# Batch norm after a matmul: w loaded by single blocks of k, x's first chunk by halves of k

## The chip, the cores and the metric

The kernel runs on one core of a Trainium2 chip. The metric is the device time of one execution in microseconds (us), beside a profile of one execution that gives each engine's instructions: TensorE (PE, with its weight loads listed apart as PEld), VectorE (DVE), ScalarE (ACT), GpSimd (POOL) and SyncE (SP), and the DMA engines that move data between the chip's memory (HBM) and the core's SBUF.

## The reference

```python
batch, m, k, n = 16, 512, 1024, 768          # x [16, 512, 1024], weight [1024, 768], fp32
def reference(x, weight, gamma, beta, eps):
    y = np.matmul(x, weight)
    mean = np.mean(y, axis=(0, 1), keepdims=True)
    var = np.var(y, axis=(0, 1), keepdims=True)
    y_norm = (y - mean) / np.sqrt(var + eps)
    return (gamma * y_norm + beta).astype(np.float32)
```

So 8192 rows of x times a 1024 x 768 matrix, and then each of the 768 columns normalised over all 8192 rows. No column of the output can be written before all rows of that column are known.

## The kernel before

**Tiling.** The 8192 rows are 16 chunks (C) of 512 rows (CH), each of two halves (QPC) of 256 rows (QR). The 768 columns are six tiles of 128 (NT). The first two tiles (GA = 2, 256 columns, NA) are called rows: for them x is the stationary operand, a group of 128 rows is multiplied with 256 columns of w, and the result has rows on the partitions. The other four tiles are called columns: w is stationary and 512 rows stream past. The contraction over k = 1024 is cut in four quarters of 256 (KQ), one on each group of 32 partitions, and inside a quarter in four blocks of 64 (jw, JW = 4) of two elements each side by side (e). One product over all of k is thus eight matmuls, two for each block. Block jw needs all four quarters of w's block jw, and all four quarters of x's block jw.

**Loading.** POOL issues the loads of w and x, which turn fp32 into bf16 on the way. One load moves one quarter: 32 partitions. `load_w(jw, jw1, quarters)` loads some blocks of w into `w_sb` (L387), `load_x(m0, rows, slot, between)` loads rows of x into a slot of `ring` (L403), four loads each. The ring holds three chunks. At most eight of POOL's loads are under way: each new one waits until the load eight places before it has landed (DMA lanes 0 to 7, used in turn). Before, the order is: w blocks 0 and 1 (quarters 0, 1), the first 256 rows of x, w blocks 0 and 1 (quarters 2, 3; the table `BETWEEN`), the next 256 rows, w blocks 2 and 3, then chunk 1 by 256 rows, and chunks 2 to 15 by 512 rows, the last in two pieces.

**Transposes.** `turn_x` (L428, L435) turns a slot of the ring on DVE into `xT_sb`, with k on the partitions. For chunk 0 this is done by halves of the rows and halves of k (two blocks), four transposes of [128 x 512 words]; the other chunks are turned by halves of the rows alone.

**Products.** `mm_rows` (L510) makes the rows tiles, `mm` (L575) the columns tiles. For chunk 0, `part(0, 1, [0, 1])` multiplies the first 256 rows with blocks 0 and 1, `part(1, 2, [0, 1])` the next 256, and then blocks 2 and 3 follow for all 512 rows. `wake` (L591) makes products of a tile of zeros, eight ahead of everything (`WAKE`), followed by eight small ones, and one (`FILL`; two passes in the profile) between the two parts. Chunk 1 has all its rows products and then all its columns products.

**After a product.** For the rows tiles ACT squares the result (L659), DVE adds it to a sum (L662), POOL or DVE adds the squares (L666), and ACT keeps a bf16 copy (L672). For the columns tiles DVE or ACT takes statistics (L711, L720, L724), and a bf16 copy is kept (L715). ACT makes plain copies of some chunks of x for faster streaming (`x_pl`, L547). When all rows of a tile are known, it is normalised, turned where needed (on PE, L1044, or in SP's DMA transposes) and stored by SP. The last tile's statistics are complete after PE's last product of y (L753); its normalisation (L1348), turning, copies (L1361) and stores (L1364) are the tail.

**The order.** Every piece of work is a `Task` with a priority, the engines that may do it with planned times (time the engine is held, time until the result is there), and its inputs and buffers. `arrange` places them one by one: at each step the engine that can begin earliest takes, of the tasks that could begin within 0.2 us, the one with the first priority. `Wires` plans the DMA. The order that comes out is what each engine executes; the planned times act through the order alone. On the chip an engine goes through its own list in order and waits where an input is missing. The waits themselves are put in by the framework, from the regions of memory that instructions write and read.

Of the kernel before, what the change touches and what calls it, by code (L numbers as in the profile page):

```python
# [9 lines left out]
class Task:  # L10
# [3 lines left out]
    def __init__(self, prio, engines, emit, deps=(), dma=None, uses=(), takes=()):  # L14
        self.prio, self.engines, self.emit, self.deps = prio, engines, emit, list(deps)
        self.dma, self.uses, self.takes = dma, list(uses), list(takes)
        self.end = self.after = None
        self.hosts = 0
        self.count = 1
        self.lock = False  # L20
        self.slack = self.look = 0.0
        for slot in self.uses + self.takes:
            slot.users.append(self)
# [74 lines left out]
class Wires:  # L98
# [4 lines left out]
    def __init__(self):  # L103
        self.free = 4.3
        self.lanes = {"SP": [], "POOL": [], "ACT": []}
# [5 lines left out]
    def send(self, queue, t, hold, took, count):  # L111

        soft = queue == "POOL"
        for _ in range(count):
            t = max(t, self.ready(queue)) + hold / count
            self.free = max(self.free, t + (1.0 if soft else 0.5)) + took / count
            land = self.free + (1.3 if soft else 0.6)
# [4 lines left out]
def arrange(tasks, turns, log=None):  # L122
# [8 lines left out]
    SEM, LOOK = 0.06, 0.2  # L131
# [36 lines left out]
    while left:  # L168
# [46 lines left out]
        if t.dma:  # L215
            free[e], t.end = wires.send(e, start, occ, t.dma, t.count)
# [11 lines left out]
def kernel(  # L228
# [30 lines left out]
    FILL = 1  # L259
    SMALL = 8  # L260
    TOUCH = 1
    BETWEEN = {0: [0, 1]}
# [112 lines left out]
    STORE, XBAR = 1 / 350.0, 1.25  # L375
# [64 lines left out]
    order = [("x", 0), ("w", 0, 2), ("x", 1), ("w", 2, 4)]  # L440
    order += [("x", q) for q in range(2, SHORT * QPC)] + [("c", c) for c in range(SHORT, C - 1)]
# [6 lines left out]
    for kind, n, *n1 in order:  # L448
        if kind == "w":
            quarters = [i for i in range(4) if n > 0 or i not in sum(BETWEEN.values(), [])]  # L450
# [7 lines left out]
            continue  # L458
        rows = n1[0] if kind == "p" else QR if kind == "x" else CH
# [4 lines left out]
        between = BETWEEN if m0 == 0 else {}  # L464
        also = sum(len(v) for v in between.values())
        load = task(
            t, {"POOL": (2.68 * rows / CH + 0.535 * also, 2.68 * rows / CH + 0.535 * also)}, load_x(m0, rows, slot, between),
            dma=(rows * K * 4 / 1024 + 384 * also) * PER_KB * 1.024, takes=[slot])
        load.count = 4 + also
# [3 lines left out]
        for i in range(rows // QR):  # L473
            c, q = divmod(m0 // QR + i, QPC)
            for j0, j1 in ((0, JW // 2), (JW // 2, JW)) if m0 < CH else ((0, JW),):
                new = q == 0 and j0 == 0
                x_ready[c, q, j1] = task(
                    -1000 + t, dve((2.2 if c in SINGLE else 1.16) * (j1 - j0) / JW + 0.02),
                    turn_x(slot, x_slot[c], m0, i * QR // 32, j0, j1, new), [load],
                    uses=[slot] if new else [slot, x_slot[c]], takes=[x_slot[c]] if new else [])  # L480
                if not new:
                    x_ready[c, q, j1].deps.append(x_ready[c, 0, JW // 2 if m0 < CH else JW])
            x_ready.setdefault((c, q, JW // 2), x_ready[c, q, JW])
        if rows % QR:
# [4 lines left out]
                -1000 + t, dve(0.63), turn_x(slot, x_slot[c], m0, t0, 0, JW, False, P),  # L489
# [159 lines left out]
    def rows_stats(c, ts, slot, t):  # L649
# [30 lines left out]
        s = task((now + 4.2 if c < RC - 2 else 0), {"POOL": (1.36, 1.36 + 0.05), "DVE": (0.62, 0.7)}, add_squares, [a],  # L680
# [124 lines left out]
    def ga_unit(nt, c, q, cols=QR):  # L805
# [26 lines left out]
        b = task(clock[0] - late, dve(0.609 * cols / CH + 0.05), bn, [t], uses=[slot])  # L832
        mine = [h[1] for k, h in ga_half.items() if k[1] == c]
        k = task(clock[0] + 3.4, act(0.48 * cols / CH + 0.03), keep, [b] + mine,
                 uses=[slot] + ([y_row[c]] if mine else []), takes=[] if mine else [y_row[c]])
        ga_half[nt, c, q] = b, k

    for c in range(1, RC):
        for ts in ([0, 1], [2, 3]):
            rows_unit(c, ts)  # L840
        if c in PARTED:
            part_chunk(c, clock[0] + (4.0 if c < EARLY else 20.0), act(1.05))
        columns = ([c - 1] if 0 < c - 1 < EARLY and c - 1 in PARTED else []) + (
            [c] if c < EARLY and c not in PARTED else [])
# [10 lines left out]
    merges.append(task(U, dve(0.36), merge(0), [k[1] for k in ends], True))  # L855
    merges.append(task(U, pool(0.65), merge(1), [k[2] for k in ends]))
    for h in range(2):
        merges.append(task(U, pool(0.65), more(h), merges[1:]))
# [59 lines left out]
    s1 = task(U, pe(0.9), sums_rows, merges, takes=[tot_slot])  # L918
    se = task(U, dve(0.8), sums_entry, [s1], True, uses=[tot_slot])
    ag = [task(U, dve(0.25), aggregate_rows(a), [se] + [h[0] for k, h in ga_half.items() if k[0] == a]) for a in range(GA)]  # L920
    rt = task(U, {"ACT": (0.2, 0.3)}, root_rows, ag)
    sc = task(U, dve(0.3), scale_rows, [rt], True)
    sr = task(U + 0.1, dve(0.35), shift_rows, [sc], True)
    p0 = task(U, pe(0.45), spread_rows(0), [sc], takes=[a0_slot])
    p1 = task(U, pe(0.45), spread_rows(1), [sr], takes=[a1_slot])
    p1.look = 0.6
    sh = task(U, act(0.3), shift_sbuf, [p1], uses=[a1_slot])


    def rows_out(c, s0, s1, k):  # L930
# [19 lines left out]
        a = task(due, dve(0.3 * n), norm, [p0] + keeps, takes=[slot], uses=[y_row[c], a0_slot])  # L950
# [461 lines left out]
```

## Time and profile before

| | us |
|---|---|
| median of 3 runs (lowest, highest) | 205.97 (205.72, 206.15) |
| profiled execution, span from first to last instruction | 204.07 |
| PE busy | 189.3 (93%), 1210 products |
| DVE busy | 159.3 (78%) |
| ACT busy | 146.2 (72%) |
| POOL busy | 124.1 (61%) |
| HBM read, written | 36.71 MB, 25.17 MB |

The page cuts the span into 40 slices of 5.1 us; a digit is the busy share in tenths, PEclk the granted clock of TensorE, DMA the busy share of the 16 DMA engines:

```profile
PE   7969999999999999999999999999999999997900
DVE  4031879999999999969989998987999878657900
PEclk9999999999999999999999999999999999999965
DMA  4999999999999999999686899899999999999998
GB/s 71 172 199 196 176 196 196 196 197 197 190 193 197 197 196 196 196 197 195 103 181 200 297 339 336 248 301 328 295 322 227 336 303 274 347 343 310 310 347 253
```

The first half of the span loads x (some 196 GB/s as written in bf16, twice that as read in fp32), the second half stores. GB/s counts the bytes written.

### The profile page before, as it was taken

The page shows a single profiled execution, that of the slowest core. Times are in us where ns is not written, and L with a number is a line of the kernel's source. Part 1 is how long each engine was busy: PE and PEld are TensorE (multiplying, and loading weights), DVE is VectorE, ACT ScalarE, POOL GpSimd, SP SyncE. Part 2 cuts the span into 40 slices and gives each one's busy share as a digit, 9 for nine tenths or more (in the row PEclk, how much of TensorE's full clock was granted, in tenths as well). Part 3 has the DMA queues.
Part 4 walks back from the last instruction along what each step waited for, and adds up shares of the span by engine and source line. Part 5 has one row for each costly group of instructions (what it writes and reads, how often), then busy time and mean ns, then how long its engine had stood idle before and what let it go on. Part 6 is the DMA issues. An engine that isn't in the chain of part 4 may idle for free.

```text
span 204.1 us, 3510 instructions
## 1 busy us (share of the span) xinstructions
PE 189.3 (93%) x1210; PEld 114.5 (56%) x1210; DVE 159.3 (78%) x250; ACT 146.2 (72%) x260; POOL 124.1 (61%) x150
## 2 busy tenths in 40 slices
PE   7969999999999999999999999999999999997900
PEld 3457554657488888777865444444444445544600
DVE  4031879999999999969989998987999878657900
ACT  2001461368989999899978766999998959956950
POOL 7776954877499989997403999389613312940000
PEclk9999999999999999999999999999999999999965
DMA  4999999999999999999686899899999999999998
GB/s 71 172 199 196 176 196 196 196 197 197 190 193 197 197 196 196 196 197 195 103 181 200 297 339 336 248 301 328 295 322 227 336 303 274 347 343 310 310 347 253
DMA packets 98562, 48.74 MB, mean 239 GB/s; under 512 B 24304, under 2 KB 98032, under 8 KB 98544
## 3 DMA queue, kind: packets, MB, share of 16 engines
q0 software_dynamic: 34624, 18.36, 65.5%
q1 hardware_dynamic: 63920, 30.16, 52.6%
q8 instruction: 9, 0.15, 0.3%
q14 instruction: 9, 0.07, 0.1%
HBM read 36.71 MB, written 25.17 MB: 303 GB/s over the span
## 4 chain that ended last, share of the span: by engine, by line
PE 86%; ACT 3%; DMA 3%; POOL 2%; issue 1%; ACTq 0%; DVE 0%; POOLq 0%
PE y_ps L575 54%; PE y_ps L510 24%; PE y_ps L814 4%; ACT o_sb L1361 3%; DMA ring<-in_x_dram 3%; PE o_ps L1044 1%; POOL ring L403 1%; POOL w_sb L387 1%; PE y_ps L753 1%; PE a_ps L903 1%; PE o_ps L1074 0%; ACTq L1407 0%; PE idle_ps L591 0%; PE tot_ps L871 0%; ACT ring L1252 0%
## 5 line engine op out<-in xcount | busy, mean ns | idle before, releaser
L575 PEld LDWEIGHTS <-w_sb 128*128 128x128 bf16 x520 | 50.3, 97 | 57.6
L575 PE MATMUL y_ps<-xT_sb,w_sb 128*128 128x512 bf16 (+1 forms) x272 | 59.3, 371 | 0.0
L575 PE MATMUL y_ps<-x_pl,w_sb 128*128 128x512 bf16 x248 | 57.4, 379 | 0.0
L403 POOL DMA_DIRECT2D ring<-in_x_dram x76 | 47.2, 626 | 14.4 <-DMA ring<-in_x_dram 5.5
L510 PE MATMUL y_ps<-w_sb,xT_sb 128*128 128x256 bf16 x448 | 50.6, 273 | 1.7 <-DMA ring<-in_x_dram 1.6
L510 PEld LDWEIGHTS <-xT_sb 128*128 128x128 bf16 x448 | 43.5, 98 | 9.4 <-DVE xT_sb L435 2.9
L435 DVE STREAM_TRANSPOSE xT_sb<-ring 128x1024 f32<-128x1024 f32 (+1 forms) x29 | 31.2, 1111 | 14.1 <-DMA ring<-in_x_dram 13.9
L711 DVE BATCH_NORM_STATS2 stats<-y_ps 128x6 f32<-128x512 f32 x46 | 30.9, 687 | 7.7 <-PE y_ps L575 7.2
L715 ACT CAST y_sb<-y_ps 128x512 bf16<-128x512 f32 x51 | 29.0, 593 | 10.4 <-DVE stats L711 6.3
L547 ACT COPY x_pl<-xT_sb 128x1024 bf16<-128x1024 bf16 x32 | 32.8, 1063 | 1.7 <-DVE xT_sb L435 1.7
L942 POOL TENSOR_TENSOR ring<-ring,sum 128x1024 f32<-128x1024 f32 (+1 forms) x11 | 23.8, 2188 | 14.9 <-ACT y_ps L724 10.9
L659 ACT ACTIVATE sq_sb<-y_ps 128x512 f32<-128x512 f32 x28 | 16.3, 610 | 16.2 <-PE y_ps L510 15.9
L666 POOL TENSOR_TENSOR sum<-sum,sq_sb 128x512 f32<-128x512 f32 x20 | 25.6, 1278 | 3.0 <-ACT sq_sb L659 1.7
L662 DVE TENSOR_TENSOR sum<-y_ps,sum 128x512 f32<-128x512 f32 x28 | 18.9, 675 | 6.3 <-ACT sq_sb L659 5.3
L672 ACT CAST y_sb<-y_ps 128x512 bf16<-128x512 f32 x28 | 16.3, 594 | 8.2 <-DVE sum L662 8.0
L1178 POOL TENSOR_TENSOR ring<-ring,sum 128x1024 f32<-128x1024 f32 x6 | 14.8, 2477 | 9.8 <-issue 8.5
L937 DVE TENSOR_TENSOR ring<-y_sb,a_ps 128x1024 f32<-128x1024 bf16 (+1 forms) x16 | 16.7, 1079 | 0.1
L1044 PE MATMUL o_ps<-ident,y_sb 128*128 128x128 bf16 x104 | 13.1, 221 | 1.6 <-DVE y_sb L1348 1.5
L1232 ACT CAST ring<-ring 128x1024 f32<-128x1024 bf16 x13 | 13.8, 1063 | 0.6 <-DMA ring<-y_sb 0.6
L1145 POOL COPY sum<-sum 32x256 f32<-32x256 f32 (+1 forms) x17 | 5.8, 340 | 13.4 <-DVE sum L1142 6.5
L428 DVE STREAM_TRANSPOSE xT_sb<-ring 128x2048 bf16<-128x2048 bf16 x6 | 13.5, 2290 | 0.1
L591 PE MATMUL idle_ps<-idle_sb 128*128 128x512 f32 x18 | 9.6, 688 | 1.5 <-DVE idle_sb L316 1.5
(104 smaller groups left out, 153.7 us busy)
## 6 DMA issues: line engine op xcount, KB each, us to landing
out_dram<-ring SPq DMA_DIRECT2D x37, 512.0 KB, 3.4
ring<-in_x_dram POOLq DMA_DIRECT2D x52, 256.0 KB, 8.8
out_dram<-o_sb SPq DMA_DIRECT2D x6, 512.0 KB, 4.7
ring<-in_x_dram POOLq DMA_DIRECT2D x16, 128.0 KB, 5.9
w_sb<-in_weight_dram POOLq DMA_DIRECT2D x8, 192.0 KB, 6.2
out_dram<-ring SPq DMA_DIRECT2D x6, 256.0 KB, 3.0
ring<-in_x_dram POOLq DMA_DIRECT2D x4, 192.0 KB, 7.8
out_dram<-o_sb SPq DMA_DIRECT2D x3, 256.0 KB, 2.5
```

Source lines behind the costliest of these rows:

```text
L403: bi = seq(nc.gpsimd.dma_start(x_bf[32 * i:32 * i + 32], src[:, :, KQ * i:KQ * (i + 1)]))
L435: seq(nc.vector.transpose(dst, src[:, :, jw0:jw1]))
L510: seq(nc.tensor.matmul(y_ps[:, s], x_of(c, jw, e, t * P, (t + 1) * P), w_sb[:, jw, e, 0:NA], start=(s == 0 and jw == 0 and e == 0), stop=( ...
L547: seq(nc.scalar.copy(dst, pairs) if eng == "ACT" else ENG[eng].tensor_copy(dst, pairs))
L575: seq(nc.tensor.matmul(y_ps, w_sb[:, jw, e, nt * P:(nt + 1) * P], moving(c, jw, e, q0 * QR, q1 * QR, parted), start=(jw == 0 and e == 0 an ...
L659: seq(nc.scalar.activation(sq_sb[:, 0:n], slot.tile[:, 0:n], AF.Square))
L662: seq(nc.vector.tensor_add(sum1, slot.tile[:, 0:n], sum1))
L666: seq(ENG[eng].tensor_add(acc, acc, state["sq"][:, 0:n]))
L711: seq(nc.vector.bn_stats(dst, slot.tile))
L715: seq(nc.scalar.copy(y(nt, c), slot.tile))
L937: seq(nc.vector.tensor_mul(slot.o, y_row[c].y[:, s0:s1], aff[0][:, None, :].to_broadcast([P, n, NA])))
L942: seq(ENG[eng].tensor_add(slot.o, slot.o, row[:, None, :].to_broadcast([P, n, NA])))
```

## The change

w is loaded in four steps of one block each, four loads a step (16 loads instead of 8). Chunk 0 of x is loaded in two steps, each with all 512 rows and half of every quarter of k (blocks 0 and 1, then 2 and 3), four loads a step, into one ring slot: rows of 128 elements where there were 256. `BETWEEN` and `FILL` are gone. Chunk 0 is multiplied with block 0 by halves of the rows, then with blocks 1, 2 and 3, one at a time, over all rows. Chunk 1 is transposed by halves of the rows and of k, and multiplied half by half. The planned times of most tasks, and those of the DMA plan, take other values.

```diff
@@ class Wires
-        self.free = 4.3
+        self.free = 4.21
-    def send(self, queue, t, hold, took, count):
-        soft = queue == "POOL"
+    def send(self, queue, t, hold, took, count, turned=False):
+        if turned:
+            t = max(t, self.ready(queue))
+            self.free = max(self.free, t + 0.722) + took
+            land = max(self.free + 0.375, t + hold + 1.4)
+            self.lanes[queue].append(land)
+            return max(t + hold, land - 2.325), land
+        first, last = (1.095, 1.0425) if queue == "POOL" else (0.722, 0.441)
...
-    SEM, LOOK = 0.06, 0.2
+    SEM, LOOK = 0.03, 0.2
...
-    FILL = 1
-    BETWEEN = {0: [0, 1]}
...
-    def load_x(m0, rows, slot, between):
+    def load_x(m0, rows, slot, k0=0, k1=KQ):
         def emit(eng):
-            x_bf = piece(slot).bitcast(bf16).rearrange("p (t k) -> p t k", k=KQ)
-            slot.tile = x_bf
+            if k0 == 0:
+                slot.tile = piece(slot).bitcast(bf16).rearrange("p (t k) -> p t k", k=KQ)
             src = x_flat[m0:m0 + rows].rearrange("(t r) k -> r t k", r=32)
             for i in range(4):
-                for quarter in between.get(i, ()):
-                    load_quarter(quarter, 0, 2)
-                bi = seq(nc.gpsimd.dma_start(x_bf[32 * i:32 * i + 32], src[:, :, KQ * i:KQ * (i + 1)]))
+                bi = seq(nc.gpsimd.dma_start(
+                    slot.tile[32 * i:32 * i + 32, :, k0:k1], src[:, :, KQ * i + k0:KQ * i + k1]))
...
-    order = [("x", 0), ("w", 0, 2), ("x", 1), ("w", 2, 4)]
-    order += [("x", q) for q in range(2, SHORT * QPC)] + [("c", c) for c in range(SHORT, C - 1)]
+    order = [("w", 0, 1), ("k", 0), ("w", 1, 2), ("k", 1), ("w", 2, 3), ("w", 3, 4)]
+    order += [("x", q) for q in range(QPC, SHORT * QPC)] + [("c", c) for c in range(SHORT, C - 1)]
...
+        if kind == "k":
+            slot = Slot(rings, RT * KQ * 2) if n == 0 else slot
+            load = task(t, {"POOL": (2.6, 2.6)}, load_x(0, CH, slot, n * KQ // 2, (n + 1) * KQ // 2),
+                        dma=CH * K * 2 / 1024 * PER_KB * 1.024, **({"uses": [slot]} if n else {"takes": [slot]}))
+            load.count = 4
...
+            j0, j1 = (0, JW // 2) if n == 0 else (JW // 2, JW)
+            for q in range(QPC):
+                new = n == 0 and q == 0
+                x_ready[0, q, j1] = task(
+                    -1000 + t, dve(0.62), turn_x(slot, x_slot[0], 0, q * QR // 32, j0, j1, new),
+                    [load] + ([] if new else [x_ready[0, 0, JW // 2]]),
+                    uses=[slot] if new else [slot, x_slot[0]], takes=[x_slot[0]] if new else [])
+            continue
...
-            for j0, j1 in ((0, JW // 2), (JW // 2, JW)) if m0 < CH else ((0, JW),):
+            for j0, j1 in ((0, JW // 2), (JW // 2, JW)) if m0 < SHORT * CH else ((0, JW),):
...
-    part(0, 1, [0, 1])
-    fill_slot = Slot(banks)
-    pe_task(0.87 * FILL, wake(FILL, fill_slot), [w_ready[0]], takes=[fill_slot])
-    part(1, 2, [0, 1])
-    for h in range(2):
-        rows_unit(0, [2 * h, 2 * h + 1], [2, 3])
-    for nt in range(GA, NT):
-        col_unit(nt, 0, [2, 3])
+    for q in range(QPC):
+        part(q, q + 1, [0])
+    for jw in range(1, JW):
+        for h in range(2):
+            rows_unit(0, [2 * h, 2 * h + 1], [jw])
+        for nt in range(GA, NT):
+            col_unit(nt, 0, [jw])
...
+    for q in range(QPC):
+        for jws in halves:
+            rows_unit(1, [2 * q, 2 * q + 1], jws)
+        for nt in range(GA, NT):
+            col_unit(nt, 1, range(JW), q, q + 1)
...
-        s = task((now + 4.2 if c < RC - 2 else 0), {"POOL": (1.36, 1.36 + 0.05), "DVE": (0.62, 0.7)}, add_squares, [a],
+        s = task((now + 4.2 if c < RC - 2 else 0), {"POOL": (1.22, 1.276), "DVE": (0.60, 0.682)}, add_squares, [a],
...
-        b = task(due, {"SP": (1.4, 1.4)}, xbar, [col_end[nt, c + i][1] for i in range(GY)] + [gate], dma=XBAR,
+        b = task(due, TURN, xbar, [col_end[nt, c + i][1] for i in range(GY)] + [gate], dma=XBAR,
```

Some twenty other tasks have their planned times changed in the same manner.

More of the change, by code (lines that the diff above doesn't have):

```diff
@@ L215, in arrange @@
         if t.dma:
-            free[e], t.end = wires.send(e, start, occ, t.dma, t.count)
+            free[e], t.end = wires.send(e, start, occ, t.dma, t.count, t.turned)
         t.start, t.engine = start, e
@@ L449 @@
         if kind == "w":
-            quarters = [i for i in range(4) if n > 0 or i not in sum(BETWEEN.values(), [])]
+            quarters = range(4)
             took = len(quarters) * 192 * 4 * (n1[0] - n) / 4 * PER_KB * 1.024
@@ L463 @@
         slot = Slot(rings, rows // 32 * KQ // 2)
-        between = BETWEEN if m0 == 0 else {}
-        also = sum(len(v) for v in between.values())
         load = task(
-            t, {"POOL": (2.68 * rows / CH + 0.535 * also, 2.68 * rows / CH + 0.535 * also)}, load_x(m0, rows, slot, between),
-            dma=(rows * K * 4 / 1024 + 384 * also) * PER_KB * 1.024, takes=[slot])
-        load.count = 4 + also
+            t, {"POOL": (2.57 * rows / CH,) * 2}, load_x(m0, rows, slot),
+            dma=rows * K * 4 / 1024 * PER_KB * 1.024, takes=[slot])
+        load.count = 4
         slot.loader = load
@@ L854 @@
                 ga_unit(nt, c, q)
-    merges.append(task(U, dve(0.36), merge(0), [k[1] for k in ends], True))
-    merges.append(task(U, pool(0.65), merge(1), [k[2] for k in ends]))
+    merges.append(task(U, {"DVE": (0.489, 0.567)}, merge(0), [k[1] for k in ends], True))
+    merges.append(task(U, {"POOL": (0.70, 0.737)}, merge(1), [k[2] for k in ends]))
     for h in range(2):
-        merges.append(task(U, pool(0.65), more(h), merges[1:]))
+        merges.append(task(U, {"POOL": (0.735, 0.764)}, more(h), merges[1:]))
     S = clock[0]
@@ L1010, in finish_tasks @@
         if nt in ASTAT:
-            deps = [task(now + 1.0, {"ACT": (1.2, 1.3)}, total, deps)]
+            deps = [task(now + 1.0, {"ACT": (0.82, 0.91)}, total, deps)]
         a = task(now + 1.0, dve(0.5), var, deps)
@@ L1014, in finish_tasks @@
         if nt > GA:
[L1015 removed]
+            return task(now + 1.0, {"DVE": (0.78, 0.87)}, affine, [b], True)
         d = task(now + 1.0, dve(0.1), invert, [b])
@@ L1270 @@
             for i, c in enumerate(LATE):
-                part_chunk(c, clock[0] + 0.0 + 4.0 * i, {"DVE": (0.63, 0.7), "ACT": (1.05, 1.1)},
+                part_chunk(c, clock[0] + 0.0 + 4.0 * i, {"DVE": (0.58, 0.67), "ACT": (0.946, 1.056)},
                            i == 0, 4.0 / 4, [col_end[NT - 3, late[-1]][1]])
```

73 lines of the change are left out of this document (39 added, 34 removed).

## The prediction

> **What bounds the kernel now.** I read the page first, then the chain of waits, then the timeline of single engines over the first 30 us, then windows over the tail. The page gives PE 189.3 us busy of a span of 204.1 (93%), and the chain that ended last is 86% PE. In the chain of waits (start us, us, what) the beginning is this:
>
> ```profile
> 5.98 6.13 DMA ring<-in_x_dram
> 12.11 0.03 issue
> 12.14 1.03 PE y_ps L510 x8
> 13.17 1.81 PE y_ps L575 x16
> 14.99 0.86 PE idle_ps L591 x2
> 15.85 0.87 PE y_ps L510 x8
> 16.72 1.81 PE y_ps L575 x16
> 18.54 0.07 issue
> 18.61 1.91 PE y_ps L510 x16
> 20.51 3.61 PE y_ps L575 x16
> 24.12 1.76 PE y_ps L510 x16
> ...
> 186.62 0.24 PE o_ps L1044 x4
> ```
>
> The first real product starts at 12.14, and from there to 186.62 the chain stays on PE, with 0.07 and 0.04 us between pieces. So the span is: start of PE's work, plus PE's work, plus a tail of 204.07 - 186.62 = 17.45 us. Inside lies 0.86 us of idle products. PE's waits, in total, times, longest, agree: after its first product nothing holds it until the last normalisation.
>
> ```profile
> PE y_ps L510 <- DMA ring<-in_x_dram: 1.6, 1, 1.6
> PE o_ps L1044 <- DVE y_sb L1348: 1.5, 1, 1.5
> PE idle_ps L591 <- DVE idle_sb L316: 1.5, 1, 1.5
> ```
>
> Therefore each us by which PE's work starts later, or is interrupted, ends up in the span, and what moves on another engine costs nothing until PE waits for it. DVE's timeline shows when x can be used (start, us, idle before and its releaser):
>
> ```profile
> 10.26 1.30 DVE L435 STREAM_TRANSPOSE xT_sb<-ring 128x512 f32<-128x512 f32 x2 [7.13 <-DMA ring<-in_x_dram]
> 14.85 1.30 DVE L435 STREAM_TRANSPOSE xT_sb<-ring 128x512 f32<-128x512 f32 x2 [3.28 <-DMA ring<-in_x_dram]
> 20.31 0.69 DVE L662 TENSOR_TENSOR sum<-y_ps,sum 128x512 f32<-128x512 f32 x1 [4.15 <-ACT sq_sb L659]
> ```
>
> The first 256 rows are usable at 10.26, the next at 14.85. At 14.85 the loads had brought 1.57 MB of w (blocks 0 and 1) and 2.10 MB of x.
>
> **Part 1: x by halves of k, and what the transposes wait for.** The new load order is w block 0, x half 0, w block 1, x half 1, w blocks 2 and 3. The intent is that PE begins after 0.79 + 1.05 MB. The built program says otherwise. The queue of POOL puts half 0 on DMA lanes 4 to 7 and half 1 on the same lanes 4 to 7, as each lane's second load. On DVE, the first transpose of chunk 0 waits for lanes 4 to 7, and the other three carry no wait at all, although two of them read half 1. They can be right only if the first wait already covers both halves: it asks for two landings on each lane. (The two halves interleave inside every row of one ring slot, so to whatever tracks overlaps they are one region.) So the halves save nothing: the first transpose waits for w0 + x0 + w1 + x1 = 0.79 + 1.05 + 0.79 + 1.05 = 3.67 MB, the same 3.67 MB that before had landed at 14.85, not the 2.62 MB that set 12.14.
>
> To 14.85 comes the price of shorter packets. Half a row is 512 bytes read and 256 written, against 1024 and 512 before, so chunk 0's x is 4096 packets instead of 2048. No row has that size. Nearest above: stores of 512-byte lines, 2711 packets in the 4 us from 196 to 200 on 16 engines, 23.6 ns each. Now: x in the window 26 to 31, 1913 packets in 5 us, 41.8 ns each. 4096 x 23.6 / 16 - 2048 x 41.8 / 16 = 6.04 - 5.35 = +0.69. Bounds: below, -0.6, since the flow dipped while x first ran (91 GB/s in 6 to 7 us against 206 in 8 to 9), beside POOL's identity work that now comes later; above, +5.35, a short packet costing as much as a long one. I take 0.7, by the row nearest in size. The DMA_TRANSPOSE packets (3620 of some 250 bytes from 102 to 107, up to 293 GB/s, which is 14 ns each) show no such doubling.
>
> The Trainium skill (DMA: Bandwidth & Descriptors, Specifications) names 512 bytes as the least transfer for line rate, with read-modify-write below; by that rule chunk 0's x would take twice as long and the sum would be near the upper bound. The transposes' 256-byte packets in this trace speak against it; it is the third rival.
>
> First transpose: 14.85 + 0.7 = 15.55. Before, PE's weight load followed 0.77 after such a start (14.85 to 15.62), so PE starts at 16.32. Before, its effective start was 12.14 + 0.86 (idle products) + 0.07 = 13.07. Difference: **+3.25 us**; the 0.86 that the change removes is in this number.
>
> **Part 2: the clock.** PE's idle products end at 10.56. The gap to the first product was 1.58 us; it becomes 16.32 - 10.56 = 5.76. The trace shows both edges. At the start, weight loads of the same kind take 0.34 until 4.21 and 0.19 from 4.80, after a first product at 1.49; at the end, PE's last product ends at 194.09 and the granted clock falls between 195.6 and 195.8 (first fence PE's weight loads in order of time; second the windows, where the third number from the end is the granted clock, before DMA share and GB/s):
>
> ```profile
> 4.21 0.34 PEld L591 LDWEIGHTS idle_ps<-idle_sb 128*128 128x128 f32 x1 [0.52 <-issue]
> 4.80 0.19 PEld L591 LDWEIGHTS idle_ps<-idle_sb 128*128 128x128 f32 x1 [0.25 <-issue]
> ```
>
> ```profile
> 195.40:195.60 0.20, 0.00 (x0) 0.00 (x0) 0.00 (x0) 0.20 (x1) 0.00 (x0) 1.00 1.16 351
> 195.60:195.80 0.20, 0.00 (x0) 0.00 (x0) 0.00 (x0) 0.20 (x1) 0.00 (x0) 0.68 1.14 346
> ```
>
> So about 1.6 idle us were enough to lose the clock there, and some 3 busy us (1.49 to between 4.21 and 4.80) were needed to have it. With 5.76 idle I expect half speed for the first 3 us: **+1.5 us** (2.7 to 3.3 us at half speed lose 1.35 to 1.65). Bounds: 0 if the clock holds; 2.9 if it needs twice the start's time. Nothing hides it: by then all of chunk 0 is close behind in SBUF.
>
> The Trainium skill (TensorE: Matmul & The Clock Gate, Part 1) puts the judging in free-running windows of about 3.4 us, and shows one loss 5.2 us after the last product; by the 5.2 the clock would fall just before PE starts, with the same loss. That rule only spreads the number from run to run.
>
> **Part 3: the order at chunk 0's end.** The new plan puts both row sums of chunk 0 on DVE ahead of chunk 1's transposes; before, one sum and a square-add stood there. From the start T of block 3's products: its first rows end T + 0.44, square on ACT 0.61 with 0.08 latency to T + 1.13, sum 0.69 to T + 1.85, second sum to T + 2.5, then a transpose of 0.65 and 0.12 to PE: T + 3.27. PE has 0.87 + 1.81 = 2.68 of work in block 3 and wants it at T + 2.7. **+0.55 us**. Bounds 0 (the two sums overlap as 20.31 and 20.91 did) and 1.2. Going on in the same way through chunks 1 to 3 I find no further wait; the closest, an ACT keep before the rows of chunk 3, has 0.4 us to spare.
>
> **Parts at nothing.** w by single blocks: 16 issues instead of 8, 8 x 0.55 = 4.4 us more of POOL, in place of some 3.5 us that POOL sat waiting for landings between 5.98 and 18.75; chunk 1's x is issued about 2.5 us later, hidden by PE being in chunk 0 until 28.9. Uncovered it would cost the 2.5. Products of 256 columns where 512 stood (32 to 80, 488 to 464): 16 of 256 take 1.81 and 16 of 512 take 3.61, so the same per column. Four chunk-1 transposes of 0.65 for two of 1.24: DVE, +0.1, ahead of PE. Two x_pl copies move from ACT to DVE and four square-adds from DVE to POOL; PE waited for neither engine. On POOL chunk 0's two square-adds (1.28 each) now stand ahead of chunk 3's loads and wait for PE's block 3: those loads are issued near 29.8 instead of 23.37. PE needs chunk 3 some 24 us after T = 26, so it is covered; late next is the end of the load stream, in the fourth rival. The other planned durations alter orders after that, not work; the tail's order is the same.
>
> **Sum.** 3.25 + 1.5 + 0.55 = 5.3. Span 204.07 + 5.3 = 209.4; the median of the runs, 205.97, lies 1.9 above the profiled span, so **211.3 us**, own range 210.2 to 212.8.
>
> **Rivals.** First, *the halves work* (the other side): the first transpose goes when half 0 is in, at 10.26 + 0.35. PE starts at 11.4, needs 2.72 a block, waits 0.6 for w block 2, meets the same 0.55 and reaches chunk 1 near 23.2 against 24.12: 0.95 faster, 205.0. For it: w0 + x0 are the same 1.84 MB that had landed at 10.26. Against: the missing waits on DVE. It decides if the first transpose starts below 14. Second, *the clock holds* over 5.76 us: 209.8; for it, the 1.58 gap did not lose it; against, the tail. Third, *short packets cost as much as long ones*: +5.35 instead of 0.7, 215.9. Fourth, *the load stream falls behind*: before, PE starts its last two groups on the last chunk at 104.94 - 1.8 = 103.1, loads ending near 98.6. Now 108.4, against 98.6 + 0.7 + 6.4 = 105.7. If one more load waits 4 us behind a square-add and a transpose's 0.7 follows, PE loses 2.0: 213.3. Against: after chunk 3 PE is what everything follows, so the queues wait as planned.
>
> **Chances.** Forecast 0.60, halves work 0.06, clock holds 0.13, short packets 0.08, load stream 0.13. The range 209.2 to 214.2 covers the forecast, most of the clock case and the load case, about 0.8. Under 0.2% (0.4 us) this kernel's runs, 205.72 to 206.15, can't be told from no change. Only the first rival is faster: 0.05, same 0.01 (its upper end), slower 0.94.
>
> **What would show it.** Right: one group of four chunk-0 transposes starting at 15 to 16, PE's first product near 16.3, first products at twice their length, a PE wait near 0.5 at chunk 1, and no PE wait after. Wrong: two groups of transposes (10.6 and 15.5); first products of 256 columns at 0.11 us each at once; x of chunk 0 landing past 18; PE waits near 100 to 108.

## The result, and the profile after

The changed kernel takes 216.06 us (median of 6 runs, 213.76 to 216.66) against 206.06 us of the kernel before in the same session (205.59 to 206.62): a ratio of 1.0464, 95% interval 1.0423 to 1.0504. It is slower by 10.0 us; 5.3 were forecast, and 216 lies outside the range. The profiled execution has a span of 214.5 us (its run took 216.24). Medians and ratios in this document leave out executions over 1.5% above the fastest of the same kernel; there is one, of e1 (215.51).

First the beginning. DVE's timeline of the changed kernel (start us, us, what, count, idle before and its releaser), then PE's; the lines of the transposes are L439 now, the rows' products L528, the columns' L593:

```profile
16.22 2.49 DVE L439 STREAM_TRANSPOSE xT_sb<-ring 128x512 f32<-128x512 f32 x4 [13.09 <-DMA ring<-in_x_dram]
```

```profile
16.99 1.03 PE L528 MATMUL y_ps<-w_sb,xT_sb 128*128 128x256 bf16 x4 [5.33 <-DVE xT_sb L439]
17.82 1.91 PE L593 MATMUL y_ps<-xT_sb,w_sb 128*128 128x256 bf16 x8
...
20.38 1.08 PE L593 MATMUL y_ps<-xT_sb,w_sb 128*128 128x256 bf16 x8
...
30.08 1.92 PE L528 MATMUL y_ps<-w_sb,xT_sb 128*128 128x256 bf16 x16 [0.59 <-DVE xT_sb L439]
```

All four transposes of chunk 0 stand in one group, behind one wait: nothing was begun with half 0 alone. PE waits 5.33 us, and its first eight column products take 1.91 us where the same eight take 1.08 at 20.38. The windows say why; the third number from the end is the granted clock:

```profile
16.00:20.00 4.00, 3.01 (x15) 2.09 (x16) 2.49 (x4) 0.30 (x1) 3.53 (x8) 0.62 1.03 160
20.00:24.00 4.00, 3.94 (x27) 2.60 (x27) 0.00 (x0) 0.00 (x0) 3.19 (x6) 0.95 1.09 132
```

Chunk 1 begins on PE at 30.08 instead of 24.12: 5.96 us late, about what the forecast had for the whole. But PE's last group, 64 transposes, begins 10.41 late, and the tail behind it is as long as it was (15.5 us). First the group before, then after:

```profile
188.59 5.50 PE L1044 MATMUL o_ps<-ident,y_sb 128*128 128x128 bf16 x64 [1.53 <-DVE y_sb L1348]
```

```profile
199.00 5.50 PE L1066 MATMUL o_ps<-ident,y_sb 128*128 128x128 bf16 x64 [1.53 <-DVE y_sb L1372]
```

So another 4.45 us went between chunk 1 and the end. PE's waits in total, times and longest, without the two that the kernel before has too (its idle products' and the last normalisation's); between its first product and the last normalisation that kernel had none:

```profile
PE y_ps L528 <- DVE xT_sb L439: 6.7, 3, 5.3
...
PE o_ps L1096 <- DVE y_sb L1086: 1.1, 1, 1.1
PE a_ps L925 <- DVE scale L917: 0.8, 1, 0.8
PE o_ps L1066 <- DVE y_sb L1048: 0.5, 1, 0.5
PE y_ps L831 <- DVE xT_sb L439: 0.3, 1, 0.3
```

After chunk 1 they lie at 98.3 (0.78, x), 104.9 (0.30, x), 115.7 (0.78), 120.2 (1.06) and 179.6 (0.46): 3.38 of the 4.45 us. The other 1.07 is in no wait of a quarter of a us or more. The first two are waits for x, so I went to POOL, which issues its loads; its timeline there:

```profile
82.44 5.35 POOL L684 TENSOR_TENSOR sum<-sum,sq_sb 128x512 f32<-128x512 f32 x4
87.74 5.12 POOL L406 DMA_DIRECT2D ring<-in_x_dram  x8
```

Four square-adds in a row hold back eight loads for 5.35 us, after a group of three from 70.43. In the page's row of GB/s the flow falls from 197 to 178, 175, 154 and 163 in the slices from 75 to 97, where the kernel before holds 196 to 197 (a slice is 5.4 us here):

```profile
GB/s 61 165 170 159 133 192 153 192 197 196 194 190 197 197 178 175 154 163 195 182 36 202 179 309 310 320 316 352 306 306 256 312 334 283 343 345 256 276 347 258
```

The chain of waits has the end of it:

```profile
97.26 10.16 DMA ring<-in_x_dram
107.55 0.93 DVE xT_sb L439
...
110.30 4.35 DMA r_sb<-y_sb
...
120.47 0.56 PE o_ps L1096 x7
```

The last of x comes so late that the transposing DMAs, which SP starts only behind it, begin late too; ACT and DVE wait for those, and PE for them (the waits at 115.7 and 120.2). That is the fourth rival of the prediction, with a larger price, and the experiments had to say what in the change makes it.

When so many MB of w and x had landed (us, added up from the packets of each trace; runs e3 to e12 are told below):

| MB landed | before | after | e3 | e9 | e11 | e10 | e12 |
|---|---|---|---|---|---|---|---|
| 3.67 (chunk 0 and half of w) | 13.50 | 14.78 | 14.40 | 14.74 | 14.37 | 13.73 | 13.61 |
| 7.34 (chunk 1) | 22.96 | 26.81 | 25.64 | 26.71 | 26.46 | 24.91 | 22.79 |
| 28.3 | 77.18 | 82.97 | 81.72 | 82.86 | 82.25 | 79.00 | 77.10 |
| 36.6 (of 36.7) | 98.78 | 106.85 | 103.36 | 104.75 | 106.13 | 100.63 | 98.62 |

In "after" the stream is 5.8 us behind at 28.3 MB, as PE is, and 8.1 at 36.6.

### The profile page after: what moved, and what is told of

Its sections match the earlier page's. It is cut to its first block, busy times and chain, and to the rows that moved or that the text cites. A ratio compares the mean times of both kernels' runs of the same rounds, so it can differ in the third digit from the quotient of the medians.

```text
span 214.5 us, 3553 instructions
## 1 busy us (share of the span) xinstructions
PE 191.3 (89%) x1218; PEld 117.5 (55%) x1232; DVE 159.3 (74%) x250; ACT 144.9 (68%) x264; POOL 131.3 (61%) x156
## 3 DMA queue, kind: packets, MB, share of 16 engines
q0 software_dynamic: 36800, 18.36, 65.3%
## 4 chain that ended last, share of the span: by engine, by line
PE 45%; DMA 16%; DVE 13%; POOL 10%; ACT 8%; issue 3%; ACTq 1%; POOLq 0%; DVEq 0%
PE y_ps L593 31%; DMA ring<-in_x_dram 13%; PE y_ps L528 11%; POOL ring L406 6%; DVE stats L729 4%; DMA r_sb<-y_sb 3%; ACT o_sb L1385 3%; DVE x_pl L565 3%; POOL sum L684 2%; DVE y_sb L1048 2%; PE o_ps L1066 2%; ACT x_pl L565 1%; ACT sq_sb L677 1%; POOL w_sb L392 1%; DVE xT_sb L439 1%
## 5 line engine op out<-in xcount | busy, mean ns | idle before, releaser
L593 PEld LDWEIGHTS <-w_sb 128*128 128x128 bf16 x544 | 53.1, 98 | 55.2
L593 PE MATMUL y_ps<-xT_sb,w_sb 128*128 128x512 bf16 (+1 forms) x289 | 60.1, 358 | 0.4
L528 PE MATMUL y_ps<-w_sb,xT_sb 128*128 128x256 bf16 x448 | 51.9, 275 | 6.8 <-DVE xT_sb L439 6.7
L593 PE MATMUL y_ps<-x_pl,w_sb 128*128 128x512 bf16 x241 | 56.8, 379 | 0.3
L528 PEld LDWEIGHTS <-xT_sb 128*128 128x128 bf16 x448 | 43.8, 98 | 14.6 <-DVE xT_sb L439 8.1
L406 POOL DMA_DIRECT2D ring<-in_x_dram x76 | 47.7, 636 | 6.1 <-DMA ring<-in_x_dram 3.4
L439 DVE STREAM_TRANSPOSE xT_sb<-ring 128x1024 f32<-128x1024 f32 (+1 forms) x31 | 31.2, 1047 | 20.9 <-DMA ring<-in_x_dram 20.7
L684 POOL TENSOR_TENSOR sum<-sum,sq_sb 128x512 f32<-128x512 f32 x24 | 31.0, 1293 | 10.1 <-ACT sq_sb L677 9.3
L729 DVE BATCH_NORM_STATS2 stats<-y_ps 128x6 f32<-128x512 f32 x46 | 30.4, 683 | 5.4 <-PE y_ps L593 5.3
L964 POOL TENSOR_TENSOR ring<-ring,sum 128x1024 f32<-128x1024 f32 (+1 forms) x11 | 23.8, 2185 | 16.4 <-DVE ring L959 16.3
L733 ACT CAST y_sb<-y_ps 128x512 bf16<-128x512 f32 x51 | 28.5, 592 | 7.5 <-DVE stats L729 3.9
L565 ACT COPY x_pl<-xT_sb 128x1024 bf16<-128x1024 bf16 x30 | 30.3, 1063 | 1.8 <-DVE xT_sb L439 1.8
L690 ACT CAST y_sb<-y_ps 128x512 bf16<-128x512 f32 x28 | 15.4, 607 | 3.3 <-DVE sum L680 3.2
```

Of the source, the lines that this page charges most:

```text
L406: bi = seq(nc.gpsimd.dma_start(slot.tile[32 * i:32 * i + 32, :, k0:k1], src[:, :, KQ * i + k0:KQ * i + k1]))
L439: seq(nc.vector.transpose(dst, src[:, :, jw0:jw1]))
L528: seq(nc.tensor.matmul(y_ps[:, s], x_of(c, jw, e, t * P, (t + 1) * P), w_sb[:, jw, e, 0:NA], start=(s == 0 and jw == 0 and e == 0), stop=( ...
L565: seq(nc.scalar.copy(dst, pairs) if eng == "ACT" else ENG[eng].tensor_copy(dst, pairs))
L593: seq(nc.tensor.matmul(y_ps, w_sb[:, jw, e, nt * P:(nt + 1) * P], moving(c, jw, e, q0 * QR, q1 * QR, parted), start=(jw == 0 and e == 0 an ...
L684: seq(ENG[eng].tensor_add(acc, acc, state["sq"][:, 0:n]))
```

## The experiments

All times are medians; the kernel before took 205.89, 205.92 and 206.00 us beside them in the three sessions.

### Which half of the change costs what: e3 and e2

e3 keeps the changed loads and products and puts back the planned durations; e2 keeps the kernel before and takes the new durations. Their core (of some 40 such lines):

```diff
-        self.free = 4.21
+        self.free = 4.3
...
-    SEM, LOOK = 0.03, 0.2
+    SEM, LOOK = 0.06, 0.2
...
-        s = task((now + 4.2 if c < RC - 2 else 0), {"POOL": (1.22, 1.276), "DVE": (0.60, 0.682)}, add_squares, [a],
+        s = task((now + 4.2 if c < RC - 2 else 0), {"POOL": (1.36, 1.36 + 0.05), "DVE": (0.62, 0.7)}, add_squares, [a],
```

> The changed kernel's loads (single w blocks, k-halves in one slot) with the planned durations of the kernel before. The start is that of the changed kernel: PE's first product near 17, chunk 1 near 30. Theory A (the late 4.4 us follow from the late start): they stay, 213.5 to 217. Theory B (they come from the order that the new durations make): they go, the last of x lands near 103, no PE wait over 0.5 between 90 and 125, 210.5 to 212.5.

> The kernel before with its own loads, and only the changed planned durations put in (which change the order of work on the queues: 24 square-adds on POOL instead of 20). The start is that of the kernel before: first product near 12.1, chunk 1 near 24. Theory A (all loss follows from the start): 204.5 to 207. Theory B (POOL's queue under the new durations is enough to let the load stream fall behind by itself): the last of x lands past 104, PE waits near 95 to 115, 208 to 211.

e3: 211.25 us, ratio 1.0257 (1.0230 to 1.0284). e2: 207.39, ratio 1.0084 (1.0057 to 1.0110). With the old durations the late loss is gone entirely. e3's PE waits, all but the two that the kernel before has:

```profile
PE y_ps L521 <- DVE xT_sb L432: 5.4, 2, 4.9
```

These are 4.85 before the first product and 0.58 at chunk 1; nothing follows. PE is 5.11 late at chunk 1 and 5.16 late at its last group. So the loads and products cost 5.4 us, and the durations, whose only effect is another order and another share-out of the same work, cost the other 4.8. Alone they cost 1.5 (e2), between the two forecasts. But e2 does not test what its expectation says: its plan puts 20 square-adds on POOL, as before, not 24, and its stream is on time (36.6 MB in at 99.0). The 1.5 is thus another cost of the durations than a late stream, and whether POOL's new order would harm the loads of the kernel before was not tested.

### What in the order does it: e5, e7, e9, e11

POOL's queue, written as loads (l) and square-adds (a), from the middle of the input on: "after" has a3 l4 a2 l4 **a4 l8** a2 l4 a2 l4 a1, e3 has a2 l4 a2 l4 a2 l4 a2 l4 a2 l4 a1 l4 a1; in all 24 square-adds against 21. First the one duration that could decide it, put back in "after" (e5), and put in alone over e3 (e7):

```diff
e5
-... {"POOL": (1.22, 1.276), "DVE": (0.60, 0.682)}, add_squares, [a],
+... {"POOL": (1.36, 1.36 + 0.05), "DVE": (0.62, 0.7)}, add_squares, [a],
```

> The changed kernel with one planned duration put back: the square-add's (POOL 1.36, DVE 0.62 as before, instead of 1.22 and 0.60). The plan then puts 22 of them on POOL instead of 24, but keeps the group of four square-adds followed by eight loads that fills POOL from 82 to 93 in the changed kernel. Theory B1 (what is lost after chunk 1 is lost in POOL's queue, each square-add there holding back the loads behind it by 1.29): 2 x 1.29 = 2.6 less of it if their number counts, 212.5 to 213.7; if the group of four ahead of eight loads is what counts, 215 to 216. Theory B2 (the other new durations, of statistics, normalisation and stores, are what costs the late 4.8): 215 to 216.5.

> The converse: the changed kernel's loads with the planned durations of the kernel before, except the square-add's, which is the new one. The plan puts 23 square-adds on POOL, with a group of four ahead of eight loads. Theory B1: the loss is back, last of x near 106 to 107 (103.4 with 21 square-adds), 213.5 to 216. Theory B2: as with all old durations, 211 to 211.8.

e5: 214.83 (1.0409, 1.0346 to 1.0472), e7: 215.18 (1.0471, 1.0397 to 1.0545). Two square-adds fewer brought about 1.2 us in e5, not 2.6, and the interval overlaps that of "after"; its queue still had the group of four ahead of eight loads. In e7 one duration alone, which makes that group, brought 3.9 of the 4.8 back in the median. Its executions are far apart (214.02 to 216.99), and the profiled one, the fastest, shows less: PE's last group is 1.19 later than in e3, and another 1.26 is in the tail. So number and group had to be parted. e9 leaves the changed kernel's plan as it is, with 24 square-adds, and only moves loads forward in it; e11 takes e3 and moves one load back:

```diff
     order = arrange(tasks, turns)
e9
+    loads = [t for t in order if is_load(t)]
+    for before, load in list(zip(loads, loads[1:]))[5:]:
+        between = [t for t in order[order.index(before):order.index(load)] if is_add(t)]
+        if len(between) > 2:
+            at = max(earliest(load), order.index(between[2]))
+            order.insert(at, order.pop(order.index(load)))
e11
+    load = [t for t in order if is_load(t)][-4]
+    adds = [t for t in order if is_add(t) and order.index(t) > order.index(load)][:2]
+    order.insert(order.index(adds[1]), order.pop(order.index(load)))
```

> The changed kernel, its plan and all its 24 square-adds on POOL, but loads of x moved ahead in POOL's queue so that two square-adds at most (three once) stand between loads, where the changed kernel has groups of three and four and eight loads after the four. Theory G (the grouping ahead of loads is what lets the load stream fall behind late): last of x at 104 to 105 instead of 106.85, no or half the PE waits near 98 to 105, 212.3 to 214. Theory N (the number of square-adds counts, or other orders of the plan): last of x near 106.5, 215 to 216.5.

> The converse: the changed kernel's loads with the planned durations of the kernel before (211.25, last of x at 103.36, 21 square-adds), with one load of four issues moved behind two more square-adds, so that once four square-adds stand ahead of eight loads, as in the changed kernel. Theory G: last of x 2 us later, near 105.4, some PE waits after 95, 212.3 to 214. Theory N: 211 to 211.7, the later loads catch up.

e9: 213.25 (1.0352, 1.0325 to 1.0379), 2.8 less than "after". e11: 213.91 (1.0397, 1.0369 to 1.0426), 2.7 more than e3. Each interval is clear of that of the kernel it was made from. POOL's timeline of e11, and PE's line that answers to it:

```profile
80.10 2.64 POOL L677 TENSOR_TENSOR sum<-sum,sq_sb 128x512 f32<-128x512 f32 x2
84.55 2.64 POOL L677 TENSOR_TENSOR sum<-sum,sq_sb 128x512 f32<-128x512 f32 x2 [1.81 <-ACT sq_sb L670]
87.14 5.11 POOL L399 DMA_DIRECT2D ring<-in_x_dram  x8
```

```profile
98.38 3.67 PE L521 MATMUL y_ps<-w_sb,xT_sb 128*128 128x256 bf16 x32 [1.45 <-DVE xT_sb L432]
```

Here the loads stand behind square-adds that in turn wait 1.81 us for ACT's squares, which wait for PE: 7.04 us from 80.10 to the next load. One load in another place of POOL's queue, with no work added, costs 2.7 us in the median; x's 36.6 MB are in at 106.13 instead of 103.36. Of PE's 2.35 us between e3's and e11's last groups, 1.45 is this wait, and 0.66 was there at chunk 1 already (chunk 0's landing differs from run to run).

In e9 the same plan without the group has 36.6 MB in at 104.75, and PE's waits at 98.3, 115.7 and 120.2 are gone; 0.67 at 104.7 (the line below) and 0.38 at 176.8 remain:

```profile
PE y_ps L831 <- DVE xT_sb L439: 0.7, 1, 0.7
```

e9 is still 2.0 above e3. Its trace puts 1.23 of its 2.51 us to chunk 1's start and 1.05 to these two waits; which of the other orders make the rest (its three square-adds more than e3's among them), and how much of the late start is only this run's, stays open.

A group is not a harm in every stream. The kernel before has three square-adds, eight loads, and three square-adds again, and its flow stays at 196 to 197: POOL still waits 0.74 us for a landing among these loads, a sign that they were issued early enough.

```profile
64.16 3.98 POOL L666 TENSOR_TENSOR sum<-sum,sq_sb 128x512 f32<-128x512 f32 x3
68.08 3.84 POOL L403 DMA_DIRECT2D ring<-in_x_dram  x6
...
73.48 0.64 POOL L403 DMA_DIRECT2D ring<-in_x_dram  x1 [0.74 <-DMA ring<-in_x_dram]
```

### What in the loads costs the 5.4: e1, e6, e4

e1 and e6 give the two k-halves ring slots of their own, with the new durations (e1) and the old (e6):

```diff
-            if k0 == 0:
-                slot.tile = piece(slot).bitcast(bf16).rearrange("p (t k) -> p t k", k=KQ)
+            slot.tile = piece(slot).bitcast(bf16).rearrange("p (t k) -> p t k", k=k1 - k0)
...
-            slot = Slot(rings, RT * KQ * 2) if n == 0 else slot
+            slot = Slot(rings, RT * KQ)
+            slot.jw0 = n * JW // 2
```

> The changed kernel, with the two k-halves of chunk 0 in two ring slots of their own instead of interleaved in one; the order of instructions on every engine is that of the changed kernel, only what the transposes wait for differs. Theory A (everything follows from the late start: the shared slot makes the first transpose wait for both halves, the clock is lost in the wait, and the later PE waits near 98 to 120 come from the loads being pushed back by the same few us): two groups of transposes of chunk 0, near 10.7 and 15 to 16; PE's first product at 11.3 to 12 and at full speed at once; chunk 1 begins on PE near 24 (30.1 in the changed kernel), and the time is 204.5 to 206. Theory B (the late 4.4 us have a cause of their own: POOL's queue, with 24 square-adds instead of 20 and 8 more load issues, lets the load stream fall behind whatever the start was): the start is as in A, but the PE waits near 92 to 114 remain, the last of x lands 6 us or more after the 98.6 of the kernel before, and the time is 208.5 to 210.5.

> The k-halves in two ring slots and the planned durations of the kernel before. In the run with two slots and new durations PE began at 11.41, waited 1.68 for w block 2 and 2.67 for chunk 1, which began at 26.80 with its clock gone (24.12 in the kernel before). If POOL's queue is all that was lost later: 2.7 for the start, 0 to 1.5 for the clock, nothing after: 208.5 to 210.3. If the single blocks cost more than their issue (8 more loads that each wait for one of 8 outstanding to land), chunk 1 stays near 26.8 here too, though PE has been free since 23.9.

e1: 212.40 (1.0321, 1.0300 to 1.0342). e6: 209.10 (1.0164, 1.0115 to 1.0214). The slot is worth 3.7 us with the new durations and 2.2 with the old. Both forecasts of e1 missed: neither had PE, once early, wait 1.68 for w and 2.67 for chunk 1's x, as its profile shows. e6's first two transposes on DVE (the other two follow at 15.76), and the first and the last of its pieces on PE up to chunk 1 that waited for x:

```profile
10.90 1.31 DVE L432 STREAM_TRANSPOSE xT_sb<-ring 128x512 f32<-128x512 f32 x2 [7.76 <-DMA ring<-in_x_dram]
```

```profile
11.67 0.61 PE L522 MATMUL y_ps<-w_sb,xT_sb 128*128 128x256 bf16 x4 [0.50 <-DVE xT_sb L432]
...
25.73 3.15 PE L522 MATMUL y_ps<-w_sb,xT_sb 128*128 128x256 bf16 x16 [2.52 <-DVE xT_sb L432]
```

Now the first half is transposed at 10.90, and PE begins at 11.67 at full speed, 1.4 ahead of the 13.07 from which the kernel before runs without a break. And yet it loses: it runs into chunk 1's x and waits 2.52 us, which costs the clock as well (sixteen products take 3.15 instead of 1.92); ahead of that it waits 0.47 for w. What the prediction called hidden is bare as soon as PE is early.

e4 keeps the changed kernel and only lengthens the idle products from 8 to 13:

```diff
-    WAKE = 8
+    WAKE = 13
```

> The changed kernel with 13 idle products ahead of the first real one instead of 8, all other orders the same, so that PE is busy nearly up to its first product near 17 and keeps its clock. If 1.5 us of the start's loss is the clock's, the first products take 0.11 us (256 columns) at once instead of twice that, and chunk 1 begins near 28.6 instead of 30.1. Theory A and B: if the later loss is of PE's own lateness it shrinks with it, 214.5; if the load stream sets the later part by itself, PE waits that much longer near 98 to 120 and the time stays at 215 to 216.5. If the clock was not the cause, the first products are slow still.

e4: 215.32 (1.0460, 1.0419 to 1.0501).

```profile
15.95 0.61 PE L528 MATMUL y_ps<-w_sb,xT_sb 128*128 128x256 bf16 x4 [1.10 <-DVE xT_sb L439]
...
27.43 1.92 PE L528 MATMUL y_ps<-w_sb,xT_sb 128*128 128x256 bf16 x16 [0.58 <-DVE xT_sb L439]
```

From first product to chunk 1 it takes 11.48 us, against 13.09 in "after" (16.99 to 30.08): the clock costs 1.6. PE is 2.65 earlier at chunk 1 (1.04 of it because x landed earlier in this execution) and 3.25 earlier at its last group, but the time is only 0.7 less, which the intervals don't part from nothing. In the profiled execution the rest is in the tail: for the last 1.8 us the stores flow at 20 to 24 GB/s, where "after" holds some 345 to the end.

### The loads one by one: e8, e10, e12

Each takes e6 and changes only the list of loads:

```diff
e6     order = [("w", 0, 1), ("k", 0), ("w", 1, 2), ("k", 1), ("w", 2, 3), ("w", 3, 4)]
e8     order = [("w", 0, 1), ("k", 0), ("w", 1, 2), ("k", 1), ("w", 2, 4)]
e10    order = [("w", 0, 2), ("k", 0), ("k", 1), ("w", 2, 3), ("w", 3, 4)]
e12    order = [("w", 0, 2), ("k", 0), ("k", 1), ("w", 2, 4)]
```

> As the run with two slots and old durations, but w blocks 2 and 3 in one load each quarter (4 issues instead of 8), so that chunk 1's x is issued some 2 us earlier. If the issues of single blocks are what delays chunk 1 behind an early start: chunk 1 begins near 24.5 to 25 instead of 26.8, no clock lost, 206 to 208, a wait for w's second pair of blocks near 16.8 to 18.5 in exchange. If not: as the run with two slots, 208.5 to 210.3.

> A version meant to beat both: blocks 0 and 1 of w in one load as in the kernel before, then chunk 0's x by halves of k in two ring slots, then blocks 2 and 3 of w singly; planned durations of the kernel before. First product near 12.3 (the same 2.62 MB as before must land), no idle products; blocks 0 and 1 last till 17.7, w block 2 (4.46 MB landed near 15.8, usable 1 us later) is in time, block 3 too, and chunk 1 begins at 23.3 to 24.2 against 24.12: 205 to 206. If the 8 smaller loads hold up chunk 1's x as in the run with two slots (x of chunk 1 usable at 25.5 there), chunk 1 begins near 25 and the time is 206.5 to 208.

> The same with blocks 2 and 3 of w in one load, so that there are as many loads ahead of chunk 1's x as in the kernel before. PE waits for blocks 2 and 3 (5.24 MB, landed near 17.6, usable near 18.7) 0.5 to 1.5 us from 17.7 on; chunk 1 begins at 23.6 to 24.7: 205.3 to 206.7.

e8: 208.93 (1.0142, 1.0091 to 1.0193). e10: 207.65 (1.0062, 1.0045 to 1.0079). e12: 206.11 (1.0002, 0.9991 to 1.0012). In e8 chunk 1's x is in time, but w's second half is not, so that it gains nothing clear over e6; of PE's timeline in e8:

```profile
19.61 1.03 PE L522 MATMUL y_ps<-w_sb,xT_sb 128*128 128x256 bf16 x8 [2.50 <-DMA w_sb<-in_weight_dram]
20.48 3.54 PE L587 MATMUL y_ps<-xT_sb,w_sb 128*128 128x512 bf16 x8
24.76 1.97 PE L587 MATMUL y_ps<-xT_sb,w_sb 128*128 128x512 bf16 x8
```

e10 and e12 differ in how w's second half is loaded, by eight issues or by four, and in what the planner makes of it; by 1.5 us. Windows of both (first e10, then e12; the last number is GB/s):

```profile
16.00:20.00 4.00, 3.94 (x24) 2.20 (x24) 0.06 (x1) 0.00 (x0) 4.00 (x9) 1.00 1.12 158
20.00:24.00 4.00, 3.77 (x23) 1.98 (x22) 1.07 (x2) 1.09 (x2) 2.78 (x5) 1.00 1.18 135
```

```profile
16.00:20.00 4.00, 3.54 (x22) 1.96 (x21) 0.11 (x1) 0.00 (x0) 2.86 (x5) 1.00 1.30 192
20.00:24.00 4.00, 4.00 (x24) 2.09 (x22) 2.58 (x4) 1.67 (x3) 3.58 (x7) 1.00 1.43 188
```

With the small loads the flow is 158 and 135 GB/s, without them 192 and 188, and chunk 1 has landed at 24.91 against 22.79. POOL's queue shows part of the reason: chunk 1's first x is issued at 15.42 in e10, and at 12.76 in e12, with four loads fewer ahead of it (first e10, then e12).

```profile
15.42 5.83 POOL L398 DMA_DIRECT2D ring<-in_x_dram  x10
```

```profile
12.76 1.30 POOL L398 DMA_DIRECT2D ring<-in_x_dram  x2 [0.21 <-issue]
```

Before 15.42 the small loads of e10 wait 0.2 to 0.3 us each, mostly for an earlier landing. From there POOL issues ten loads without a gap, 0.58 us each: in that stretch its own issue time holds it, not the number of loads that may be under way. Whether the lower flow has a further cause stays open. PE begins chunk 1 in time in e10 (23.70), and meets the late x further on, by way of DVE and ACT, in an execution that is the slowest of its eight (209.20):

```profile
29.16 1.07 PE L587 MATMUL y_ps<-xT_sb,w_sb 128*128 128x256 bf16 x8 [0.81 <-ACT y_sb L727]
...
47.72 3.65 PE L522 MATMUL y_ps<-w_sb,xT_sb 128*128 128x256 bf16 x32 [1.72 <-ACT y_sb L727]
```

e12 is the version nearest to the idea: x by halves, block by block, no idle products between. On PE:

```profile
12.64 0.61 PE L522 MATMUL y_ps<-w_sb,xT_sb 128*128 128x256 bf16 x4 [1.18 <-DVE xT_sb L432]
...
18.58 1.03 PE L522 MATMUL y_ps<-w_sb,xT_sb 128*128 128x256 bf16 x8 [0.40 <-DMA w_sb<-in_weight_dram]
...
23.93 1.91 PE L522 MATMUL y_ps<-w_sb,xT_sb 128*128 128x256 bf16 x16
```

Chunk 1 begins at 23.93 against 24.12, and the time is that of the kernel before. It doesn't beat it: where the kernel before has 0.86 us of idle products, e12 begins 0.5 later (12.64 against 12.14) and waits 0.40 for w's second half. That the first half of x is enough to begin with gains it nothing here.

## Why the prediction was right and wrong

**What bounds the kernel: right.** In "after", PE's last group is 10.41 us later and the span 10.4 longer; in e3 it is 5.16 and 5.7.

**Part 1, the shared slot: right, with a term too small.** One group of transposes, at 16.22 (15.55 forecast; 15.2 to 16.3 in the runs with this loading), first product 16.99 (16.32). e6 shows that the slot was the cause. The 0.7 over 14.85 became 1.37 in "after", and single blocks of w, which the prediction put at nothing, are in it. Where w's first half comes in pairs of blocks (e12, e10) chunk 0's x comes in the same short packets, and 3.67 MB are in at 13.61 and 13.73, against 13.50 before. Where it comes singly it is 14.2 to 14.8.

The 0.1 between e12 and the kernel before is not the price of the packets, though. Windows from 4 to 12 of the kernel before, then of e12 (the last number is GB/s):

```profile
4.00:8.00 4.00, 4.00 (x10) 1.86 (x9) 0.00 (x0) 0.30 (x1) 3.40 (x8) 1.00 1.13 157
8.00:12.00 4.00, 2.56 (x13) 1.10 (x11) 1.30 (x2) 0.00 (x0) 2.74 (x5) 1.00 1.27 200
```

```profile
4.00:8.00 4.00, 4.00 (x8) 1.74 (x7) 0.00 (x0) 0.30 (x1) 3.84 (x8) 1.00 1.16 183
8.00:12.00 4.00, 3.46 (x16) 1.52 (x14) 0.13 (x1) 0.00 (x0) 2.88 (x5) 1.00 1.75 172
```

While the short packets come, e12's flow is 172 against 200 with packets of 512 bytes and w's longer ones, and it makes up for that earlier, where the kernel before has the dip that the prediction named. At these two rates chunk 0's 1.05 MB (as written) differ by 0.9 us, an estimate, near the 0.7 forecast. This also answers the third rival, which had +5.35. By the rule of the Trainium skill (DMA: Bandwidth & Descriptors, Specifications) transfers below 512 bytes lose line rate: here the loss is a seventh of the flow, not half of it.

**Part 2, the clock: right.** 1.6 measured by e4, 1.5 forecast.

**Part 3, the row sums: right in size.** 0.59, forecast 0.55. It is 0.58 in e3 as well, so the new durations are not needed for it; in e10 it is 0.23, and e12, with the same products, has none.

The three parts make 5.3 in the sum; the kernel that has them alone, e3, is 5.4 slower, and 5.11 late at chunk 1 (5.96 in "after", where x came later).

**Parts at nothing: the step that failed.** It has two statements. "The other planned durations alter orders after that, not work" was taken for harmless: with the share-out between the engines, these orders cost 4.8 us. I had followed PE's, DVE's and ACT's queues through chunk 3, had found that four square-adds move from DVE to POOL, and had priced them by asking whether PE waits for POOL. It doesn't; it waits for x, whose loads stand in that queue. Where four square-adds came together in an already late stream, they held eight loads (e9, e11: 2.7 to 2.8 us for the grouping). The other 2.0 of the 4.8 is not traced to single orders. The other statement, that chunk 1's later x is hidden, holds only because PE was late itself: e6 waits 2.52 us for it, and e10, with chunk 1 landed 2.1 us later than in e12, takes 1.5 longer.

**The fourth rival was the right mechanism, but an alternative to the forecast instead of a part of it, and too small.** It had one load behind one square-add and 2.0 us; what came was a stream 8.1 us late, and 4.45 us on PE beyond the start, of which 2.92 are traced to late x. Its argument against, "after chunk 3 PE is what everything follows, so the queues wait as planned", was wrong in the traces: from 65.3 to 100.5 POOL's queue has no gap, so it follows its own work there, not PE.

Step by step back from "after": old durations -4.8 (e3), two slots -2.2 (e6), w by pairs of blocks, one ahead of chunk 0's x and one behind it, -3.0 (e12), the kernel before -0.1.

## What to carry to other kernels

A queue that issues loads and also computes must be judged by its loads: ask of every operation that a new plan puts there which transfer stands behind it and when the last byte of the input then comes, through to the end of the stream and not only through the first stages. Work that is "hidden" behind a late engine is hidden no longer once that engine is early, so an edit that starts the bound engine sooner needs the later loads sooner as well. And two parts of one buffer that are to be used one after the other need to be two regions for whatever tracks them; splitting loads finely has a price on the queue that issues them, since each load more delays all that stand behind it.

## What the runs showed of the hardware that was not expected

- Packets of 256 bytes lowered the flow of loads by a seventh (172 GB/s in e12 against 200 before, from 8 to 12 us), not by half.
- PE's clock outlasted idle gaps of 1.45 (e11) and 1.72 us (e10: 32 products at 47.7 still take 3.65), and was lost after 2.50 (e8) and 2.52 (e6). In e8 it fell not at the restart but 0.9 us into it: the eight products at 19.61 take 1.03, the next eight 3.54 instead of 1.97. But no length of gap decides: the same 1.53 us that stand ahead of the last 64 transposes in the kernel before, which then take 5.50, cost the clock in e12:

```profile
188.54 6.17 PE L1060 MATMUL o_ps<-ident,y_sb 128*128 128x128 bf16 x64 [1.53 <-DVE y_sb L1364]
```

  There the granted clock is 0.51 from 190.6 to 192.6, with PE busy throughout. That agrees with the Trainium skill (TensorE: Matmul & The Clock Gate, Part 1), by which the clock is judged in windows that run on their own; it does not agree with the idle window of about 3.4 us that the same part asks for before a loss. The 1.6 us that I read off the kernel's end are no threshold.
- In e4 the last stores dribbled out at 20 to 24 GB/s for 1.8 us, in other runs for some tenths or not at all. 345 / 16 is 21.6, and the DMA share is 0.07 there: it looks as if one of the sixteen DMA engines was left alone with its queue, which no run here tested.
